# First piece's transposes at a phase end set between the third bank's products, and the transposes of C dealt 8 clock units later

## The chip, the cores and the metric

The kernel runs on one core of a Trainium2 chip. The metric is the device time of one execution in microseconds; of several executions the median is given. TensorE is called PE in the profile, VectorE DVE, ScalarE ACT, GpSimd POOL and SyncE SP.

## The reference, cut to what matters

Two layers work on 256 tokens of width 1024, all in float32. A layer adds half a SwiGLU feed-forward block (width 2816) to h, then a token mixer, then half of a second SwiGLU block. The mixer of the first layer is an S5 diagonal state-space layer, that of the second is block-sparse attention with 8 heads, which for 256 tokens is plain causal attention.

```
def reference(x, ...):
    h = x
    for layer in range(DEPTH):
        h = h + 0.5 * swiglu(rms_norm(h, ffn_norm[layer, 0]), ...)
        hn = rms_norm(h, mix_norm[layer])
        if layer % 2 == 0: h = h + s5_mixer(hn, ...)
        else:              h = h + moba_mixer(hn, ...)
        h = h + 0.5 * swiglu(rms_norm(h, ffn_norm[layer, 1]), ...)
    return h
```

The S5 layer has 64 groups of 16 channels and 64 complex states each; its matrices B and C, the powers of its diagonal and tables made of them depend on weights alone.

## The kernel before, in words

**Phases.** The work is six phases in a row, named f00, s5, f01, f10, moba and f11: four feed-forward blocks and the two mixers. Every phase reads h transposed (model width on partitions) and ends by adding its result to h. Both stand in SBUF.

**Products in three passes.** Each float32 operand is split into a rounded high part and the rest, in a format that PE multiplies at full rate, and each product is three matmuls: high by high, high by low, low by high (`mm3`, L398 to L401; L553 to L555 in the feed-forward phases after the first). The weights stream through the class `Stream`: a `raw` buffer (three of them) is filled by a DMA of SP; a *split* makes `whi` on ScalarE (L86, or L92 with the norm's gains) and `wlo` on VectorE (L87, L93). Up to nine halves of such split weights are held. `st.pump()` issues the next split if a place is free, `st.release` frees a place.

**Order.** The instructions of each engine run in the order in which the program issues them; there is no scheduler. An engine stops at an instruction whose inputs or whose buffer are not ready, and everything behind it on that engine waits too.

**A phase end.** The function `boundary` ends a phase. The result is four accumulators (PSUM banks, `pA`), one for each 128x512 piece of h: two token tiles t by two halves n of the width. The pieces are ended in an order that the next phase sets. In the feed-forward phases the last products come in three parts of three matmuls for each piece; in s5 and moba in two parts of six. The first two pieces get all parts but the last ahead of time. Then for each piece come the parts that are left, `finish` (L371, VectorE: h gets the accumulator times a scale), and the transposes of a piece for the next phase, `prep`: four 128x128 transposes by PE into a PSUM bank `pR` (L333), a copy by ScalarE to the high part (L335), a subtraction by VectorE for the low part (L336), and the squares for the norm on ScalarE (L345). There are two `pR` banks, taken in turn by every transpose of the kernel. `prep` of the last piece comes in the next phase. After s5, a `pump` follows the second and the third piece.

**The front.** During the first phase, f00, the tables of the S5 layer are built beside the feed-forward products. A counter of *clock units* is advanced by `fill` ahead of PE's products: 0.7 for each three matmuls, so 5.6 for a gate/up product of one token tile and 2.8 for a down product. The generator `tables` issues its pieces by that clock: loads at the units in `LOADS`, the powers E from unit `E_AT`, B from `B_AT`, and the four blocks of transposes of C from unit `C_AT`, 1.4 units apart. A block is four transposes by PE into a `pR` bank (L830) and two copies by ScalarE into the table `cb` (L833):

```
later = [(C_AT + 1.4 * k, c_tr) + divmod(k, 2) for k in range(4)]
...
if later and later[0][0] <= now:
    f = later.pop(0)
    f[1](*f[2:])
    done[0] += 1
```

The tables that are made of C wait in the program until all four blocks have been issued (`done`). In f00 the activations are transposed too: twice in the course of a gate/up pair, two 128x128 transposes into a `pR` bank (L497), with a copy by ScalarE (L499) and a subtraction by VectorE (L500).

Of the kernel before, what the change touches and what calls it, by code (L numbers as in the profile page):

```python
# [30 lines left out]
OO = 68  # L31

LOADS = (20, 21, 22, 23, 24, 26, 28, 30, 32, 34, 36, 38) + (44, 50, 56, 66, 76, 88, 100, 112)
C_AT, E_AT, B_AT, DENSE, LAG, PACE, AGE = 44, 26, 36, (64, 0.39, 0.46), 12, 3.5, 8.0


class Stream:
# [83 lines left out]
def trunk_kernel(ctx: ExitStack, tc, x, ffn_norm, ffn_w_gate, ffn_w_up, ffn_w_down, mix_norm,  # L121
# [17 lines left out]
    def psR():  # L139
        return pp.tile([128, 512], F32, name="pR", tag="R", bufs=2)  # L140
# [176 lines left out]
    def home(pool, ph):  # L317

        xa = pool.tile([128, 4224], F32R, name="xa")
        v = xa[:, XO[ph]:XO[ph] + 4096].rearrange("p (i k c) -> p i k c", i=2, c=256)  # L320
        return v[:, 0], v[:, 1]

    def prep(t, n, ph, sq=True):

        if (ph, "x") not in X:
            X.clear()
            X[ph, "x"] = True
            X["h"], X["l"] = home(XP[0], ph)
        hh = h[t][:, n * 512:(n + 1) * 512]
        ps = psR()  # L330
        pv = ps.rearrange("p (k c) -> p k c", c=128)
        for k in range(4):
            nc.tensor.transpose(pv[:, k, :], hh[:, k * 128:(k + 1) * 128], ident)  # L333
        xh, xl = (X[p][:, n * 4:n * 4 + 4, t * 128:t * 128 + 128] for p in "hl")
        nc.scalar.activation(xh, pv, AF.Copy)  # L335
        nc.vector.tensor_tensor(xl, pv, xh.bitcast(F32), op=OP.subtract)  # L336
        if sq:
            squares(t, n)

    def squares(t, n):  # L340
        if n == 0:
            SS[t] = sp.tile([128, 2], F32, name="ss", tag="ss", bufs=4)
        hh = h[t][:, n * 512:(n + 1) * 512]
        sq = sp.tile([128, 512], mybir.dt.bfloat16, name="sq", tag="sq", bufs=1)
        nc.scalar.activation(sq, hh, AF.Square, accum_out=SS[t][:, n:n + 1])  # L345
        if n == 1:
            v = sp.tile([128, 1], F32, name="ms", tag="ms", bufs=4)
            nc.gpsimd.tensor_tensor(v, SS[t][:, 0:1], SS[t][:, 1:2], op=OP.add)  # L348
            nc.gpsimd.tensor_scalar(v, v, 1.0 / D, EPS, op0=OP.mult, op1=OP.add)
            r = sp.tile([128, 1], F32, name="rr", tag="rr", bufs=4)  # L350
            rsq(r, v, 1)
            Rr[t] = r
# [16 lines left out]
    def finish(t, n, acc, scale):  # L369
        hh = h[t][:, n * 512:(n + 1) * 512]  # L370
        nc.vector.scalar_tensor_tensor(hh, acc, scale, hh, op0=OP.mult, op1=OP.add)  # L371

    def boundary(nxt, parts, acc, scale, mid=None, pumps=()):

        if nxt is not None and nxt[0] == "f":
            order = [(0, 0), (1, 0), (0, 1), (1, 1)]
        else:
            order = [(0, 0), (0, 1), (1, 0), (1, 1)]
        for i in range(2):
            for part in parts[:-1]:  # L380
                part(*order[i])
            if mid is not None and i == 0:
                mid()
        for i, (t, n) in enumerate(order):
            for part in parts[-1:] if i < 2 else parts:
                part(t, n)
            finish(t, n, acc[2 * t + n], scale)
            if nxt is None:
                store(t, n)
            elif i:  # L390
                prep(*order[i - 1], nxt)
            if i in pumps:
                st.pump()
# [33 lines left out]
    def store(t, n):  # L427
        hh = h[t][:, n * 512:(n + 1) * 512]
        for s in range(4):
            off, ap = rows(t, s, n)  # L430
            (nc.sync, nc.scalar)[s % 2].dma_start(bass.AP(tensor=out.tensor, offset=out.offset + off, ap=ap),
                                                  hh[s * 32:s * 32 + 32])


    def ffn(tag, nxt, hooks, fill, to_rows, to_columns):
# [91 lines left out]
        def part(j, f):  # L527
            return lambda t, n: bank_mm(acc, t, n, *AT[j], where[tag, "d", j], [f], False, (j, f) == (L, 1))

        boundary(nxt, [part(L - 1, 1), part(L, 0), part(L, 1)], acc, 0.5, lambda: tr(L, 1))  # L530
        st.release(where[tag, "d", L - 1], 1)
        for i in range(2):
            st.release(where[tag, "d", L], i)

    def ffn_w(tag, nxt, entry):
# [75 lines left out]
        def part(j, f):  # L611
            return lambda t, n: bank_mm(acc, t, n, *AT[j], where[tag, "d", j], [f], False, (j, f) == (L, 1))

        boundary(nxt, [part(L - 1, 1), part(L, 0), part(L, 1)], acc, 0.5)
        st.release(where[tag, "d", L - 1], 1)
        for i in range(2):
# [359 lines left out]
    def s5(nxt, entry):  # L976
# [209 lines left out]
        for word in plan.split():  # L1186
            step(word)
        boundary(nxt, [lambda t, n: so(2, t, n), lambda t, n: so(3, t, n, True)], acc, 1.0, pumps=(1, 2))
        for b in (2, 3):
            for i in range(2):  # L1190
# [246 lines left out]
    for i, ph in enumerate(phases):  # L1437
        nxt = phases[i + 1] if i + 1 < len(phases) else None
# [59 lines left out]
```

## Time and profile before

| what | value |
|---|---|
| median of 3 runs | 975.3 us (974.68 to 975.59) |
| the profiled execution | 974.58 us |
| its span, first to last instruction | 972.8 us |
| mean granted TensorE clock | 0.999 |
| PE, PE weight loads | 965.9 us (99%), 863.7 us (89%) |
| DVE, ACT, POOL | 690.1 us (71%), 555.7 us (57%), 211.6 us (22%) |
| mean DMA rate | 207 GB/s |

In a row of a timeline stand the start, the duration, the engine, the line of the program, the operation, out<-in, shapes and the count of merged instructions; in brackets the idle time of the engine before it and the instruction that ended it. A matmul's record is longer than the step to the next one, since matmuls overlap; its end is modelled. In a row of the view of waits stand who waited for whom, the microseconds in total, the times and the longest. A group of instructions of one line has its count, the durations in ns (smallest, median, largest) and the first and last start.

### The profile page before, as it was taken

Reading aid. Unit: us, or ns where it says so; the run is one execution under the profiler, and the core shown is the slowest. Engines: PE = TensorE matmul, PEld = TensorE weight load, DVE = VectorE, ACT = ScalarE, POOL = GpSimd, SP = SyncE. Lnnn points to the kernel's source line nnn. Section 1 sums busy time; section 2 is a strip of 40 time slices with the busy share of each in tenths; the row PEclk is TensorE's granted clock in tenths of the full one; section 3 lists DMA queues with packets and bytes.
Section 4 is the critical chain, followed back from the end, with each engine's and each line's share of the span. In section 5 each row is a group of like instructions: output and inputs, shape, how many; then the busy total and the mean of one; then the engine's idle time right before and its main releaser. Section 6 shows DMA issues by size and latency. Waiting matters only on the chain.

```text
span 972.8 us, 17168 instructions
## 1 busy us (share of the span) xinstructions
PE 965.9 (99%) x6695; PEld 863.7 (89%) x6695; DVE 690.1 (71%) x1118; ACT 555.7 (57%) x1008; POOL 211.6 (22%) x381
## 2 busy tenths in 40 slices
PE   9999999999999999999999999999999999999998
PEld 7878777888999999999899999998888899999997
DVE  5898778768886776666568766665688667766662
ACT  7655767553376565555356555554897556555540
POOL 5961889615702000000020000001440020000000
PEclk9999999999999999999999999999999999999999
DMA  8999999986756666555446755553454646656531
GB/s 287 255 308 311 286 278 289 287 298 225 269 196 194 217 198 220 182 187 184 156 134 226 241 181 186 182 194 95 171 173 131 215 132 216 220 182 207 173 131 43
DMA packets 145505, 200.91 MB, mean 207 GB/s; under 512 B 20153, under 2 KB 117521, under 8 KB 145169
## 3 DMA queue, kind: packets, MB, share of 16 engines
q1 hardware_dynamic: 138032, 188.51, 59.4%
q0 software_dynamic: 6816, 10.71, 4.2%
q8 instruction: 52, 0.85, 0.4%
q10 hardware_dynamic: 576, 0.61, 0.3%
q14 instruction: 29, 0.23, 0.1%
HBM read 183.89 MB, written 15.76 MB: 205 GB/s over the span
## 4 chain that ended last, share of the span: by engine, by line
PE 94%; DVE 3%; POOL 2%; issue 0%; ACT 0%; ACTq 0%; POOLq 0%
PE pM L554 13%; PE pM L553 13%; PE pM L555 13%; PE pA L399 9%; PE pA L401 9%; PE pA L400 9%; PE pM L399 6%; PE pM L400 6%; PE pM L401 6%; PE pR L1066 1%; DVE wlo L87 1%; PE pR L333 1%; POOL sc L686 1%; PE pA L1110 1%; PE pA L1112 1%; PE pA L473 1%
## 5 line engine op out<-in xcount | busy, mean ns | idle before, releaser
L553 PE MATMUL pM<-xa,whi 128*128 128x256 f32 x1056 | 295.7, 280 | 0.0
L554 PE MATMUL pM<-xa,whi 128*128 128x256 f32 x1056 | 294.9, 279 | 0.0
L555 PE MATMUL pM<-xa,wlo 128*128 128x256 f32 x1056 | 294.7, 279 | 0.0
L93 DVE SCALAR_TENSOR_TENSOR wlo<-raw,gT,whi 128x512 fp32r<-128x512 f32 x328 | 228.0, 748 | 68.9 <-ACT whi L92 68.7
L87 DVE TENSOR_TENSOR wlo<-raw,whi 128x1024 fp32r<-128x1024 f32 (+1 forms) x155 | 189.2, 1234 | 48.7 <-ACT whi L86 47.1
L92 ACT ACTIVATE whi<-raw,gT 128x512 fp32r<-128x512 f32 x328 | 213.7, 712 | 14.9 <-PE pA L401 14.8
L554 PEld LDWEIGHTS pM<-xa,whi 128*128 128x128 f32 x1056 | 198.5, 188 | 2.6
L553 PEld LDWEIGHTS pM<-xa,whi 128*128 128x128 f32 x1056 | 198.5, 188 | 2.3
L555 PEld LDWEIGHTS pM<-xa,wlo 128*128 128x128 f32 x1056 | 198.5, 188 | 0.0
L86 ACT ACTIVATE whi<-raw 128x1024 fp32r<-128x1024 f32 (+1 forms) x155 | 159.5, 1049 | 31.4 <-DMA raw<-in_ffn_w_up_dram 13.1
L399 PE MATMUL pA<-whi,ah 128*128 128x512 f32 x352 | 138.7, 394 | 0.0
L400 PE MATMUL pA<-wlo,ah 128*128 128x512 f32 x352 | 137.6, 391 | 0.0
L401 PE MATMUL pA<-whi,al 128*128 128x512 f32 x352 | 137.6, 391 | 0.0
L399 PE MATMUL pM<-whi,xa 128*128 128x512 f32 (+1 forms) x304 | 122.1, 402 | 0.0
L568 ACT ACTIVATE sg<-gr 128x256 f32<-128x256 f32 x66 | 27.6, 419 | 164.4 <-DVE gr L565 164.4
L400 PE MATMUL pM<-wlo,xa 128*128 128x512 f32 (+1 forms) x304 | 115.8, 381 | 0.1
L401 PE MATMUL pM<-whi,xa 128*128 128x512 f32 (+1 forms) x304 | 115.4, 380 | 0.0
L348 POOL TENSOR_TENSOR ms<-ss 128x1 f32<-128x1 f32 x10 | 1.9, 193 | 471.8 <-ACT sq L345 471.8
L401 PEld LDWEIGHTS pA<-whi,al 128*128 128x128 f32 x352 | 66.1, 188 | 14.3
L399 PEld LDWEIGHTS pA<-whi,ah 128*128 128x128 f32 x352 | 66.1, 188 | 11.6
L400 PEld LDWEIGHTS pA<-wlo,ah 128*128 128x128 f32 x352 | 66.2, 188 | 11.4
L565 DVE TENSOR_TENSOR gr<-pM,rrow 128x512 f32<-128x512 f32 x66 | 45.5, 690 | 39.4 <-PE pM L555 39.3
(271 smaller groups left out, 1230.6 us busy)
## 6 DMA issues: line engine op xcount, KB each, us to landing
raw<-in_ffn_w_down_dram SPq DMA_DIRECT2D x44, 1024.0 KB, 5.6
raw<-in_ffn_w_gate_dram SPq DMA_DIRECT2D x80, 512.0 KB, 4.0
raw<-in_ffn_w_up_dram SPq DMA_DIRECT2D x80, 512.0 KB, 5.1
raw<-in_moba_w_qkv_dram SPq DMA_DIRECT2D x12, 1024.0 KB, 5.1
TB<-dB SPq DMA_DIRECT2D x8, 768.0 KB, 6.7
raw<-in_ffn_w_gate_dram SPq DMA_DIRECT2D x16, 256.0 KB, 4.4
raw<-in_ffn_w_up_dram SPq DMA_DIRECT2D x16, 256.0 KB, 4.7
dA<-blank SPq DMA_DIRECT2D x8, 512.0 KB, 9.2
```

The lines of the kernel that those rows point to most:

```text
L86: nc.scalar.activation(hi[:, c], r[:, c], AF.Copy)
L87: nc.vector.tensor_tensor(lo[:, c], r[:, c], hi[:, c].bitcast(F32), op=OP.subtract)
L92: nc.scalar.activation(hi[:, c], r[:, c], AF.Identity, scale=g)
L93: nc.vector.scalar_tensor_tensor(lo[:, c], r[:, c], g, hi[:, c].bitcast(F32), op0=OP.mult, op1=OP.subtract)
L399: mm(o, xh, wh, start=start, stop=False)
L400: mm(o, xh, wl, start=False, stop=False)
L401: mm(o, xl, wh, start=False, stop=stop)
L553: mm(o, a, xh, start=k == 0 and i == 0, stop=False, skip_group_check=True)
L554: mm(o, a, xl, start=False, stop=False, skip_group_check=True)
L555: mm(o, b, xh, start=False, stop=k == 7, skip_group_check=True)
L565: V.tensor_tensor(gr, ps.rearrange("p (i c) -> p i c", i=2), Rr["row"][:, None, :].to_broadcast([128, 2, 256]), op=OP.mult)
L568: nc.scalar.activation(sg, gr[:, 0, :], AF.Silu)
```

## The change

Two edits. In `boundary`, the transposes of the first piece are no longer issued behind the second piece's last part and `finish`, but behind the first part of the third piece, so three matmuls later at the end of a feed-forward phase and six at the end of s5 and moba. The transposes of the second and third piece stay where they were. At the end of the kernel (`nxt` is None) nothing is transposed. And `C_AT` is 52 for 44, so the four blocks of transposes of C are issued one gate/up product and one down product later, at the same places in them.

```
-C_AT, E_AT, B_AT, DENSE, LAG, PACE, AGE = 44, 26, 36, (64, 0.39, 0.46), 12, 3.5, 8.0
+C_AT, E_AT, B_AT, DENSE, LAG, PACE, AGE = 52, 26, 36, (64, 0.39, 0.46), 12, 3.5, 8.0
...
         for i, (t, n) in enumerate(order):
-            for part in parts[-1:] if i < 2 else parts:
+            for k, part in enumerate(parts[-1:] if i < 2 else parts):
                 part(t, n)
+                if i == 2 and k == 0 and nxt is not None:
+                    prep(*order[0], nxt)
             finish(t, n, acc[2 * t + n], scale)
             if nxt is None:
                 store(t, n)
-            elif i:
+            elif i > 1:
                 prep(*order[i - 1], nxt)
             if i in pumps:
                 st.pump()
```

On PE the moved blocks are all that changes its order. On ScalarE the copies of C move with them, past the splits and the activations of the stage between; and at the end of s5 one split comes ahead of the first piece's copy and squares; there VectorE's two operations of that split come ahead of the first piece's subtraction. VectorE's order elsewhere, and the orders of POOL and SP, are as before. Two lines are added, so a line behind `boundary` has a number higher by two in the changed kernel (L399 is L401, L500 is L502, L830 is L832).

More of the change, by code (lines that the diff above doesn't have):

```diff
@@ L33 @@
 LOADS = (20, 21, 22, 23, 24, 26, 28, 30, 32, 34, 36, 38) + (44, 50, 56, 66, 76, 88, 100, 112)
-C_AT, E_AT, B_AT, DENSE, LAG, PACE, AGE = 44, 26, 36, (64, 0.39, 0.46), 12, 3.5, 8.0
+C_AT, E_AT, B_AT, DENSE, LAG, PACE, AGE = 52, 26, 36, (64, 0.39, 0.46), 12, 3.5, 8.0
 class Stream:
@@ L384, in boundary @@
         for i, (t, n) in enumerate(order):
-            for part in parts[-1:] if i < 2 else parts:
+            for k, part in enumerate(parts[-1:] if i < 2 else parts):
                 part(t, n)
+                if i == 2 and k == 0 and nxt is not None:
+                    prep(*order[0], nxt)
             finish(t, n, acc[2 * t + n], scale)
@@ L389, in boundary @@
                 store(t, n)
-            elif i:
+            elif i > 1:
                 prep(*order[i - 1], nxt)
```

## The prediction

> **What bounds the kernel now.** I read the page's busy times first, then the chain that ended last, then TensorE's waits, and last the timelines of the places that the change touches.
>
> ```profile
> PE 965.9 (99%) x6695; PEld 863.7 (89%) x6695; DVE 690.1 (71%) x1118; ACT 555.7 (57%) x1008; POOL 211.6 (22%) x381
> PE 94%; DVE 3%; POOL 2%; issue 0%; ACT 0%; ACTq 0%; POOLq 0%
> ```
>
> TensorE (PE) is busy for 965.9 of 972.8 us and carries 94% of the chain. No product and no transpose is added or dropped by the change, so it can win only what PE now waits at the moved places, and can lose only by new waits of PE. What does PE wait for? First its row in the view of waits, then the answer on line 333 (transposes of h), whose second row says what PE's weight loads or matmuls stood idle for:
>
> ```profile
> PE pR L830 <- DVE al L500: 0.8, 1, 0.8
> L333 PE MATMUL pR<-cst,h x80: 270/272/330, 204.1 to 784.9; 128*128 128x128 f32 x80
>   DVE h L371: 1.6, 3
> ```
>
> Both lines are the moved ones: one wait at the transposes of C (L830), three at those of h. Some of these idle times count the load and the matmul of one wait twice, and a matmul's end is modelled, so I price each from the starts of the products around it.
>
> **Part 1: the first piece's transposes at the phase ends.** At a phase end the four 128x512 pieces of h are finished one after another. Before, piece 1's transposes come right behind the second piece's last product. PE at the end of the first phase: the passage with the wait, then the second piece's transposes (the row between is left out), which do not wait; below them the waiting passages of the two other phase ends:
>
> ```profile
> 203.63 0.39 PE L401 MATMUL pA<-whi,al 128*128 128x512 f32 x1
> 204.12 0.66 PE L333 MATMUL pR<-cst,h 128*128 128x128 f32 x4
> 204.53 0.48 PE L399 MATMUL pA<-whi,ah 128*128 128x512 f32 x1
> ...
> 206.46 0.40 PE L401 MATMUL pA<-whi,al 128*128 128x512 f32 x1
> ...
> 207.05 0.48 PE L399 MATMUL pA<-whi,ah 128*128 128x512 f32 x1
> ...
> 483.23 0.39 PE L401 MATMUL pA<-whi,al 128*128 128x512 f32 x1
> ...
> 484.14 0.48 PE L399 MATMUL pA<-whi,ah 128*128 128x512 f32 x1
> ...
> 669.63 0.39 PE L401 MATMUL pA<-whi,al 128*128 128x512 f32 x1
> ...
> 670.54 0.48 PE L399 MATMUL pA<-whi,ah 128*128 128x512 f32 x1
> ```
>
> From the last product before to the first after: 0.90 us with the wait, 0.59 without; 0.91 and 0.91 at the two others. That is 0.31 + 0.32 + 0.32 = 0.95 us in three phase ends. The cause is VectorE's add into h (L371), two of them in one row:
>
> ```profile
> 203.37 1.38 DVE L371 SCALAR_TENSOR_TENSOR h<-pA,h 128x512 f32<-128x512 f32 x2 [1.22 <-PE pA L401]
> 206.89 0.69 DVE L371 SCALAR_TENSOR_TENSOR h<-pA,h 128x512 f32<-128x512 f32 x1 [0.76 <-PE pA L401]
> ```
>
> The first add ends at about 203.37 + 0.69 = 204.06. In the changed order three products stand between, so the transposes come up at 203.63 + 4 x 0.23 = 204.55, some 0.5 us after the add: the wait goes. (0.23 is the step from one product to the next, 70.75 to 70.98 in the rows of part 2.)
>
> What is late next? The second piece's transposes come six products later, with their add done by 204.75. For piece 1, transposes (0.6), ScalarE's copy (0.6, as in a row below) and VectorE's subtraction (an operation of the add's size, 0.7) are through at 204.55 + 1.9 = 206.5. Behind it VectorE has the third piece's add, which PE releases no sooner than 206.89 - 0.31 = 206.58. And the transposes' PSUM buffer (there are two, in turn) is wanted again by the third piece's transposes at 207.05 - 0.31 + 9 x 0.23 = 208.8. So nothing takes the wait's place.
>
> A rule to weigh here: the Trainium skill, "TensorE: Matmul & The Clock Gate", section "Step-by-step: what each phase is for", says that PE's queue pulls weight loads ahead of running matmuls. By that rule a block that waits loses its hidden load too; counting late starts alone (0.49 against 0.23 us) would give 0.26 a place and 0.17 us less in all. The whole passages measured above agree with the rule, and I use them.
>
> The two other phase ends (after the state-space and the attention layer) have six products ahead of the transposes and no wait:
>
> ```profile
> 295.79 0.39 PE L401 MATMUL pA<-whi,xa 128*128 128x512 f32 x1
> ...
> 296.38 0.48 PE L399 MATMUL pA<-whi,xa 128*128 128x512 f32 x1
> ```
>
> 295.79 to 296.38 is again 0.59, so they bring 0. After the state-space layer one weight split (two ScalarE and two VectorE operations) now comes ahead of piece 1's copies in both queues:
>
> ```profile
> 296.71 0.60 ACT L335 ACTIVATE xa<-pR 128x512 fp32r<-128x512 f32 x1 [6.39 <-issue]
> 297.81 1.33 ACT L92 ACTIVATE whi<-raw,gT 128x512 fp32r<-128x512 f32 x2
> ```
>
> ScalarE had been idle for 6.39 us, so the split can run there. If it ran no earlier than before (297.81 to 299.14), piece 1's copy would begin at 299.1 instead of 296.7; PE asks for that PSUM buffer again only at the third piece's transposes, 24 products and a block behind 296.38, near 302.3. So it costs 0 either way. The kernel's last phase end transposes nothing and is unchanged.
>
> **Part 2: the transposes of C, 8 clock units later.** They are four blocks (L830) of four transposes. PE at the second block, without a wait, and at the fourth:
>
> ```profile
> 56.00 0.39 PE L401 MATMUL pM<-whi,xa 128*128 128x512 f32 x1
> 56.23 0.60 PE L830 MATMUL pR<-cst,cn 128*64 128x128 f32 x4
> 56.59 0.48 PE L399 MATMUL pM<-whi,xa 128*128 128x512 f32 x1
> 56.90 0.39 PE L400 MATMUL pM<-wlo,xa 128*128 128x512 f32 x1
> ...
> 60.54 0.39 PE L401 MATMUL pA<-whi,al 128*128 128x512 f32 x1
> 61.68 0.63 PE L830 MATMUL pR<-cst,cn 128*64 128x128 f32 x4 [0.75 <-DVE al L500]
> 62.06 0.48 PE L399 MATMUL pA<-whi,ah 128*128 128x512 f32 x1
> 62.38 0.39 PE L400 MATMUL pA<-wlo,ah 128*128 128x512 f32 x1
> ```
>
> A block costs 0.90 - 2 x 0.23 = 0.44 us, wherever it stands. The fourth takes 62.38 - 60.54 = 1.84, so its wait is 0.94 us: it needs the PSUM buffer that a transpose of the activations filled, and VectorE, behind with the table of powers and the splits, subtracts from it (L500) only at 61.21:
>
> ```profile
> 61.21 0.41 DVE L500 TENSOR_TENSOR al<-pR,ah 128x256 fp32r<-128x256 f32 x1
> 63.24 0.79 DVE L628 TENSOR_TENSOR e<-z,z 128x256 f32<-128x256 f32 x2
> 65.48 1.23 DVE L87 TENSOR_TENSOR wlo<-raw,whi 128x1024 fp32r<-128x1024 f32 x1 [0.76 <-ACT whi L86]
> 70.10 0.42 DVE L500 TENSOR_TENSOR al<-pR,ah 128x256 fp32r<-128x256 f32 x1
> ```
>
> Each block moves exactly one gate/up product and one down product on, and the fourth again stands behind the first bank of the down product, in the buffer of an activation transpose. So the same wait can come back there. PE and ScalarE around that place:
>
> ```profile
> 68.70 0.38 PE L497 MATMUL pR<-cst,act 128*128 128x128 f32 x2
> 70.75 0.39 PE L401 MATMUL pA<-whi,al 128*128 128x512 f32 x1
> 70.98 0.39 PE L399 MATMUL pA<-whi,ah 128*128 128x512 f32 x1
> 64.39 1.06 ACT L86 ACTIVATE whi<-raw 128x1024 fp32r<-128x1024 f32 x1 [1.28 <-PE pA L401]
> 67.52 1.06 ACT L86 ACTIVATE whi<-raw 128x1024 fp32r<-128x1024 f32 x1 [0.30 <-PE pM L401]
> L833 ACT ACTIVATE cb<-pR x8: 360/377/379, 56.6 to 62.7; 64x256 f32<-64x256 f32 x8
> ```
>
> When PE reaches the product that follows the 64.39 row it is 4 x 0.44 + 0.94 = 2.70 us earlier than before. The fourth block comes up at 70.98 - 2.70 + 3 x 0.44 = 69.60. Before, L500 began 70.10 - 65.48 = 4.62 us after the first split of that stretch, and that split waited for ScalarE, which waited for PE. ScalarE's wait moves 2.70 earlier with PE (64.39 to 61.7), VectorE is free from 64.03 on, so the split begins at about 64.2 and L500 is through at 64.2 + 4.62 + 0.42 = 69.2: 0.4 us in hand. ScalarE has two pairs of C copies more between its splits (2 x 0.377 = 0.75 us each). First block: twelve products ahead of the activation transposes, 68.70 - 2.70 - 12 x 0.23 = 63.2; second: 63.2 + 0.44 + 6 x 0.23 = 65.1; each done some 0.6 later. So ScalarE has split one at 61.7 to 62.8, the first pair at 63.9, split two at 64.6, the second pair at 65.7, split three from 66.5 to 67.5, which VectorE needs at 69.2 - 0.42 - 1.2 = 67.6. That fits. The cost lies between 0 and 0.94; I take 0, by the rows of that stretch, in which VectorE stands idle for 0.76 us.
>
> The weights have more in hand: the split at 65.48 is first used by PE one whole gate/up product later, at
>
> ```profile
> 75.77 0.39 PE L399 MATMUL pM<-whi,xa 128*128 128x512 f32 x1
> 66.00:203.00 137.00, 137.00 (x742) 110.35 (x741) 107.87 (x151) 84.02 (x144) 81.10 (x103) 1.00 0.96 285
> ```
>
> 9 us after it is ready. The second row (windows by stage; the last columns are granted clock 1.00, DMA share 0.96, GB/s) shows PE busy for all of the 137 us that follow, with DMA full at 0.96.
>
> **Sum.** 0.95 + 0.94 = 1.89 us less. The profiled execution has 974.58 us, 1.8 of it around the span of 972.8; it would have 972.7. It lies 0.7 below the median of the runs, so against 975.3 the forecast is 973.4, or 0.19%. What a measurement of this kernel can tell from no change is about 0.2%, here 1.95 us: the forecast lies at that line.
>
> **Rivals.** *A: the front's wait returns.* The fourth block waits at its new place, as VectorE's chain (third split, then L500) does not come 1.3 us earlier. The bound is L500 staying at 70.52: 70.52 - 69.60 = 0.92 us, and with it the front's gain is gone: 974.3. For it: the place has the same form as before. Against it: 0.76 us of idle VectorE. The Trainium skill, "Perfetto Trace Analysis", section "Optimization Strategy", takes a repeating gap on the engine that should be saturated as a sign of too few buffers; by that rule moving the block moves the gap, and the two-deep transpose buffer would give this case. The trace bears it out only in part: three of the four blocks pass without a gap. Chance 0.10.
>
> *B: the transfers swallow the front's gain.* With DMA at 0.96 up to 203 us, PE that is 0.94 earlier could wait for weights or for the state-space tables: 974.3. Against it: 9 us in hand at 75.77 and no wait of PE in those 137 us. Chance 0.05.
>
> *C: slower.* The C copies now stand in ScalarE's queue ahead of the activation copy that L500 needs. If VectorE's order slips by all of them, L500 ends at 70.52 + 1.5 = 72.0 and PE waits 2.4 us at the fourth block: 2.4 - 1.89 = 0.5 above before, 975.8; if the later splits slip as well, more. It decides once L500 ends after 69.60 + 1.89 = 71.5. Against it: ScalarE is idle 1.28 and 0.30 us before the two splits quoted. Chance 0.07.
>
> **How the numbers follow.** The forecast has 0.78. Its centre is 0.06 us short of the 0.2% line, and the three runs shown (974.68 to 975.59) lie further below their median than above, so I split it nearly evenly: 0.43 beyond the line, 0.35 within. A and B fall within (0.15). C gives slower: 0.07, taken whole though its first price is short of the line. Faster 0.43, same 0.50, slower 0.07. The range takes the forecast less the whole scatter of the runs, 0.9, and reaches up to A and B with half of it, 0.4: 972.5 to 974.7.
>
> **What would show it.** Right: no wait of line 333 for h in the three phase ends, and each passage 0.59 us or less by its starts; the fourth L830 block with no idle time before it, near 69.6; the first phase end's transposes of h at 204.55 - 0.94 = 203.6. Wrong: an idle time in brackets at the fourth L830 naming L500, a wait of PE for a split or a table after it, or a span that ends less than 1.5 us earlier.

## The result, and the profile after

| | before | after |
|---|---|---|
| median of 19 runs each, on the same chip | 975.21 us | 972.94 us (972.39 to 975.6) |
| the profiled execution | 974.58 us | 972.72 us |
| its span | 972.8 us | 970.9 us |
| mean granted TensorE clock | 0.999 | 1.000 |

The ratio is 0.9976, with a 95% interval of 0.9969 to 0.9983, so the kernel is faster, by 0.17 to 0.31%. By the medians that is 2.27 us less (0.23%), by the profiled executions 1.86. The forecast was 973.4, in a range of 972.5 to 974.7.

The page after, in its line of busy times; then PE's whole answer in the view of waits, and the group of line 333 (the rows on transposes of h):

```profile
span 970.9 us, 17168 instructions
PE 964.9 (99%) x6695; PEld 863.7 (89%) x6695; DVE 690.0 (71%) x1118; ACT 555.3 (57%) x1008; POOL 211.7 (22%) x381
...
PE pR L1394 <- POOL ones L229: 1.0, 1, 1.0
...
L333 PE MATMUL pR<-cst,h x80: 270/272/273, 203.7 to 783.1; 128*128 128x128 f32 x80
```

PE has as many instructions as before. The row of L830 (now L832) is gone from PE's waits: the one left stands at the very start of the kernel, before its first matmul at 0.98 us, and was there before too. Line 333 has no row of idle time any more, and its longest transpose takes 273 ns where one took 330. Now the three phase ends by their starts, in the timeline of PE after; the first row of each stretch is the second piece's last product, behind which the transposes stood before:

```profile
202.81 0.39 PE L403 MATMUL pA<-whi,al 128*128 128x512 f32 x1
...
203.49 0.39 PE L403 MATMUL pA<-whi,al 128*128 128x512 f32 x1
203.73 0.60 PE L333 MATMUL pR<-cst,h 128*128 128x128 f32 x4
204.08 0.48 PE L401 MATMUL pA<-whi,ah 128*128 128x512 f32 x1
...
482.05 0.39 PE L403 MATMUL pA<-whi,al 128*128 128x512 f32 x1
...
482.73 0.39 PE L403 MATMUL pA<-whi,al 128*128 128x512 f32 x1
...
483.31 0.48 PE L401 MATMUL pA<-whi,ah 128*128 128x512 f32 x1
...
668.12 0.39 PE L403 MATMUL pA<-whi,al 128*128 128x512 f32 x1
...
668.80 0.39 PE L403 MATMUL pA<-whi,al 128*128 128x512 f32 x1
...
669.38 0.48 PE L401 MATMUL pA<-whi,ah 128*128 128x512 f32 x1
```

From the product before the transposes to the one behind them: 204.08 - 203.49 = 0.59, 483.31 - 482.73 = 0.58, 669.38 - 668.80 = 0.58 us, where the waiting passages took 0.90, 0.91 and 0.91.

The same rows tell where the time went. The second piece's last product started at 203.63, 483.23 and 669.63 before; it is 0.82, 1.18 and 1.51 us earlier now. The kernel's last product (L401 at 967.66 before, L403 after) closes the account. Two products in PE's timeline before:

```profile
50.10 0.39 PE L401 MATMUL pM<-whi,xa 128*128 128x512 f32 x1
967.66 0.39 PE L401 MATMUL pA<-whi,al 128*128 128x512 f32 x1
```

The same two in PE's timeline after:

```profile
50.20 0.39 PE L403 MATMUL pM<-whi,xa 128*128 128x512 f32 x1
965.85 0.39 PE L403 MATMUL pA<-whi,al 128*128 128x512 f32 x1
```

At 50 us, ahead of everything that the change touches, the profiled execution after is 0.10 us later. Its shift then goes +0.10, -0.82, -1.18, -1.51, -1.81. So the front gave 0.92 us and the three phase ends 0.36, 0.33 and 0.30, all of it at the four predicted places.

The front after, by PE's timeline (the fourth block of C), VectorE's and ScalarE's:

```profile
69.46 0.39 PE L403 MATMUL pA<-whi,al 128*128 128x512 f32 x1
69.69 0.60 PE L832 MATMUL pR<-cst,cn 128*64 128x128 f32 x4
...
70.36 0.39 PE L402 MATMUL pA<-wlo,ah 128*128 128x512 f32 x1
...
64.30 1.21 DVE L87 TENSOR_TENSOR wlo<-raw,whi 128x1024 fp32r<-128x1024 f32 x1
...
68.91 0.41 DVE L502 TENSOR_TENSOR al<-pR,ah 128x256 fp32r<-128x256 f32 x1
...
61.77 1.06 ACT L86 ACTIVATE whi<-raw 128x1024 fp32r<-128x1024 f32 x1 [2.25 <-PE pA L403]
63.97 0.77 ACT L835 ACTIVATE cb<-pR 64x256 f32<-64x256 f32 x2 [1.14 <-PE pR L832]
64.76 1.06 ACT L86 ACTIVATE whi<-raw 128x1024 fp32r<-128x1024 f32 x1
65.78 0.77 ACT L835 ACTIVATE cb<-pR 64x256 f32<-64x256 f32 x2
66.57 1.06 ACT L86 ACTIVATE whi<-raw 128x1024 fp32r<-128x1024 f32 x1
```

The fourth block's passage takes 70.36 - 69.46 = 0.90 us, as long as that of the second block, which did not wait before. VectorE's subtraction is through at 68.91 + 0.41 = 69.32, and the block comes up at 69.69: 0.37 us in hand.

### The profile page after: what moved, and what is told of

The parts are those of the page before. It is cut to its first block, busy times and chain, and to the rows that moved or that the text cites. A ratio compares the mean times of both kernels' runs of the same rounds, so it can differ in the third digit from the quotient of the medians.

```text
span 970.9 us, 17168 instructions
## 1 busy us (share of the span) xinstructions
PE 964.9 (99%) x6695; PEld 863.7 (89%) x6695; DVE 690.0 (71%) x1118; ACT 555.3 (57%) x1008; POOL 211.7 (22%) x381
## 4 chain that ended last, share of the span: by engine, by line
PE 94%; POOL 2%; issue 2%; DVE 1%; ACT 1%; POOLq 0%; ACTq 0%
PE pM L556 13%; PE pM L555 13%; PE pM L557 13%; PE pA L401 10%; PE pA L403 10%; PE pA L402 10%; PE pM L401 6%; PE pM L402 5%; PE pM L403 5%; PE pR L1068 1%; PE pA L475 1%; POOL qrs L306 1%; PE pR L333 1%; PE pA L1112 1%; PE pA L1114 1%
## 5 line engine op out<-in xcount | busy, mean ns | idle before, releaser
L92 ACT ACTIVATE whi<-raw,gT 128x512 fp32r<-128x512 f32 x328 | 213.5, 711 | 14.9 <-PE pA L403 14.9
L401 PE MATMUL pA<-whi,ah 128*128 128x512 f32 x352 | 138.7, 394 | 0.0
L403 PE MATMUL pA<-whi,al 128*128 128x512 f32 x352 | 137.6, 391 | 0.0
L401 PE MATMUL pM<-whi,xa 128*128 128x512 f32 (+1 forms) x304 | 122.2, 402 | 0.0
L403 PE MATMUL pM<-whi,xa 128*128 128x512 f32 (+1 forms) x304 | 115.4, 380 | 0.0
L403 PEld LDWEIGHTS pA<-whi,al 128*128 128x128 f32 x352 | 66.1, 188 | 14.3
L401 PEld LDWEIGHTS pA<-whi,ah 128*128 128x128 f32 x352 | 66.1, 188 | 11.7
```

Source lines behind the costliest of these rows:

```text
L92: nc.scalar.activation(hi[:, c], r[:, c], AF.Identity, scale=g)
L401: mm(o, xh, wh, start=start, stop=False)
L403: mm(o, xl, wh, start=False, stop=stop)
```

## The experiments

**Both edits again, and each alone.** The first is the changed kernel once more, the second has only the phase ends (`C_AT` back at 44), the third only the front (`boundary` as before, `C_AT` 52).

> The changed kernel again, beside the other three. Theory (PE's four waits go and nothing takes their place): span 1.9 us shorter than before, about 970.9, time about 1.9 to 2.3 us less. If the extra 0.4 us between the timed runs (2.27 us) and the spans (1.9 us) is real, it shows again here; if it is scatter, the difference falls near 1.9.

> Only the transposes of h are moved, C stays at 44. Theory: the three waits at phase ends go (0.33 + 0.32 + 0.32), the wait of 0.94 us at the fourth block of C stays: span 971.8, about 1.0 us less than before. Rival (the phase ends' waits come back behind the move): span 972.8.

> Only C_AT is 52, the phase ends are as before. Theory: the front's wait goes and is not given back in the 137 us of full DMA queues that follow: span 971.9, about 0.9 us less. Rival B (the transfers swallow it): products are 0.9 us earlier at 75 us, but no longer at 200 us, span 972.8. If the parts add up, this and the kernel with the transposes of h alone give together what the whole change gives.

| kernel | median, us | ratio to before (975.06), 95% |
|---|---|---|
| both | 972.91 | 0.998 (0.997 to 0.999) |
| phase ends alone | 974.08 | 0.9989 (0.998 to 0.9998) |
| front alone | 973.92 | 0.9987 (0.9978 to 0.9996) |

The parts bring 0.98 and 1.14 us, together 2.12; both bring 2.15. Each of these intervals is about 0.9 us wide on either side, so the medians alone would not show that the parts add up; the traces do. By the starts of the same products the phase ends alone go from 0.20 us later than before at 203 us to 0.77 earlier at the last product, a gain of 0.97, and the front alone goes from 0.18 later at 50 us to 0.74 earlier at 100 us, a gain of 0.92. Together that is 1.89, beside 1.91 for both edits. Neither takes the other's gain. With the front alone line 333 keeps its idle time (1.6 us in three waits for h, as before). With the phase ends alone the wait in the front stays; here is the fourth block in PE's timeline with the phase ends alone:

```profile
60.36 0.39 PE L403 MATMUL pA<-whi,al 128*128 128x512 f32 x1
61.88 0.63 PE L832 MATMUL pR<-cst,cn 128*64 128x128 f32 x4 [1.13 <-DVE al L502]
...
62.58 0.39 PE L402 MATMUL pA<-wlo,ah 128*128 128x512 f32 x1
```

The passage takes 62.58 - 60.36 = 2.22 us, where the profile of before has 1.84, though up to here the program is the same: PE came 0.18 us earlier than in that profile, and VectorE's subtraction was through 0.20 us later. The wait of 0.94 us was 1.32 in this execution.

With the front alone the starts of the same products are 0.74 us earlier at 100 us and still 0.74 earlier at 960 us. What the front gains, nothing later takes back in this profile: rival B falls.

**The fourth block alone.** Is it enough to move the block that waited? Here `boundary` is as before, and of the four blocks only the last one is issued later:

```
later = [(c, c_tr) + divmod(k, 2) for k, c in enumerate((44.0, 45.4, 46.8, 56.2))]
```

> Phase ends as before; of the four blocks of C only the fourth is issued 8 clock units later, the first three stay. Theory: only the fourth block cost anything, by its wait for the PSUM buffer, so this alone brings the same 0.9 us: span 971.9. Rival (it is the crowd of four blocks in one stretch that puts PE behind VectorE): a quarter to a half of it, span 972.3 to 972.6.

974.04 us, 0.9989 (0.9981 to 0.9998): 1.02 us less than before, as much as all four together (1.14) within what can be told apart. In its profile PE waits at none of the four blocks; the same products gain 0.91 us between 54 and 100 us. (This one profile loses 0.4 us again up to 223 us, 0.2 of it at one place at 150 us; the profile with all four blocks moved does not, and the median does not show it.) The other three need not have moved.

**Two blocks left at the old place.** Two readings of the old wait are left: four blocks crowd ScalarE and VectorE at that place, or a block there takes a `pR` bank whose turn comes too early. If it is the crowd, fewer blocks wait less; if it is the turn, what counts is which of the two banks the last block there draws. In the changed kernel, two and then only one of the blocks go back:

```
later = [(c, c_tr) + divmod(k, 2) for k, c in enumerate((46.8, 48.2, 54.8, 56.2))]   # two
later = [(c, c_tr) + divmod(k, 2) for k, c in enumerate((48.2, 53.4, 54.8, 56.2))]   # one
```

> The changed kernel, but two blocks of C are issued at clock units 46.8 and 48.2, the places of the third and fourth block of before, and two at 54.8 and 56.2. Theory (the wait comes from the turn of the two transpose buffers: the block at 48.2 gets the buffer of the activation transposes, which VectorE empties only at 61.5 to 61.9): with two blocks fewer ahead PE arrives there 0.9 us earlier than before, at about 59.9, and waits 1.8 us, twice as long as before; span 970.9 + 1.8 = 972.7. Rival (crowding): with half the blocks the wait is at most half: span 971.4 or less.

> The changed kernel, but one block of C is issued at clock unit 48.2, where the fourth of before stood, and the other three at 53.4, 54.8 and 56.2. Theory (turn of the buffers): alone there, it gets the other buffer, which has been free since 54.7, and does not wait, although it comes up even earlier (about 59.5) and VectorE is as late as ever: span 970.9. Rival (any transpose of C at that place waits for VectorE): a wait of 1.8 to 2.2 us, span about 973.

Two blocks: 975.05 us, 1.0002 (0.9993 to 1.0012), beside 974.79 before, so the whole gain of both edits is gone. One block: 972.92 us, 0.9987 (0.9977 to 0.9996), so most of the gain stays: 1.87 us by the medians. PE's and VectorE's timelines with two blocks at the old place:

```profile
59.81 0.39 PE L403 MATMUL pA<-whi,al 128*128 128x512 f32 x1
62.01 0.63 PE L832 MATMUL pR<-cst,cn 128*64 128x128 f32 x4 [1.81 <-DVE al L502]
62.39 0.48 PE L401 MATMUL pA<-whi,ah 128*128 128x512 f32 x1
...
61.54 0.41 DVE L502 TENSOR_TENSOR al<-pR,ah 128x256 fp32r<-128x256 f32 x1
```

And with one, at the same place of the program:

```profile
58.84 0.39 PE L403 MATMUL pA<-whi,al 128*128 128x512 f32 x1
59.07 0.60 PE L832 MATMUL pR<-cst,cn 128*64 128x128 f32 x4
59.43 0.48 PE L401 MATMUL pA<-whi,ah 128*128 128x512 f32 x1
...
60.88 0.41 DVE L502 TENSOR_TENSOR al<-pR,ah 128x256 fp32r<-128x256 f32 x1
```

With half the blocks the wait is twice as long: 62.39 - 59.81 = 2.58 against 0.58 us, so 2.0 us lost where the four lost 0.94. PE arrives earlier, as less stands ahead of it, and VectorE's subtraction ends no earlier for that. With one block the subtraction is as late against PE (it starts 1.8 us after the block), and PE does not wait at all. By the order of the program the first block behind the transposes of the activations draws the other bank, and the second block draws theirs, which VectorE's subtraction has yet to read. The single block is a first one. So the wait is one for a bank's turn. Crowding falls. The run with only the fourth block moved fits this: there the third block at the old place, and the fourth at the new one, are both the first behind such transposes.

**ScalarE's copies of C doubled.** Rival C was a new wait at the new place, from copies of C in ScalarE's queue. To see how near it is, each copy is made twice (the same data to the same place):

```
-            for g in range(2):
+            for g in (0, 1, 0, 1):
```

> The changed kernel with each pair of ScalarE copies of the transposed C done twice (the same data again). It tests how thin the cover of the new place is (rival C of the prediction). Theory: the second pair ends at about 68.0 instead of 66.6, so the third block, which wants that buffer at 67.2, waits about 0.8 us, and the subtraction ahead of the fourth ends at about 70.7, another 0.2: span 970.9 + 1.0 = 971.9. Rival (the new place has ample cover): span 970.9.

974.3 us, 0.9996 (0.9987 to 1.0006): 1.4 us more than the kernel with one block at the old place, measured beside it (972.92), and more than the 1.0 expected. PE's timeline, third and fourth block:

```profile
67.16 0.38 PE L499 MATMUL pR<-cst,act 128*128 128x128 f32 x2
68.34 0.62 PE L832 MATMUL pR<-cst,cn 128*64 128x128 f32 x4 [0.81 <-ACT cb L835]
68.72 0.48 PE L401 MATMUL pM<-whi,xa 128*128 128x512 f32 x1
...
70.65 0.39 PE L403 MATMUL pA<-whi,al 128*128 128x512 f32 x1
...
71.54 0.48 PE L401 MATMUL pA<-whi,ah 128*128 128x512 f32 x1
```

The third block's passage takes 68.72 - 67.16 = 1.56 us where the changed kernel has 0.57, the fourth's 71.54 - 70.65 = 0.89 where it has 0.58: together 1.30. The larger part is at the third block: the banks are taken in turn, the transposes of the activations at 67.16 stand between it and the second block, so it draws the second block's bank, of which ScalarE now makes four copies. That wait, 0.99 us, is not the one rival C named. C's own, the activations' subtraction that comes late behind the copies, is the smaller part, 0.31 us at the fourth block: the subtraction is through at 70.97 where the changed kernel has 69.32. The change stays short of both waits, and not by much: its second pair of copies is through at 65.78 + 0.77 = 66.55, and the third block comes up at 67.19.

**One product instead of three.** How far must the first piece's transposes be moved? Here they stand behind the first of the third piece's three products:

```
             for k, part in enumerate(parts[-1:] if i < 2 else parts):
+                if i == 2 and k == 0 and nxt is not None:
+                    INNER.append(lambda: prep(*order[0], nxt))
                 part(t, n)
-                if i == 2 and k == 0 and nxt is not None:
-                    prep(*order[0], nxt)
...
     def mm3(o, xh, xl, wh, wl, start, stop):
         mm(o, xh, wh, start=start, stop=False)
+        while INNER:
+            INNER.pop()()
```

> The changed kernel with the first piece's transposes behind the first product of the third piece instead of the third. Theory (only VectorE's add has to be over): they come up 0.46 us after the last product's start, the add is visible 0.49 us after it, so 0.03 us of wait are left at each of the three feed-forward ends: span 971.0. Rival (the transposes need the longer distance, by the weight loads pulled ahead): up to 0.2 us at each, span 971.5.

973.33 us, 0.9987 (0.9977 to 0.9996), where three products had 972.9 in other sets of runs. The group of line 333 and PE's timeline at the first phase end:

```profile
L333 PE MATMUL pR<-cst,h x80: 270/272/329, 203.2 to 783.4; 128*128 128x128 f32 x80
...
  DVE h L371: 0.9, 3
...
202.92 0.40 PE L403 MATMUL pA<-whi,ah 128*128 128x512 f32 x1
203.18 0.66 PE L333 MATMUL pR<-cst,h 128*128 128x128 f32 x4
203.59 0.48 PE L406 MATMUL pA<-wlo,ah 128*128 128x512 f32 x1
```

The three waits come back, smaller: 203.59 - 202.92 = 0.67 us, 0.08 more than the 0.59 without a wait, where I expected 0.03. One more product (0.23 us) would have covered that; it was not tried.

**A next step: four waits in the attention layer.** With the waits of this change gone, PE's weight loads still wait for VectorE's splits four times in the attention layer; it did so before the change too (1.8 us in four). The view of waits of PE's weight loads after, and the first such place in PE's timeline:

```profile
PEld pM L402 <- DVE wlo L93: 1.9, 4, 0.5
...
687.89 0.39 PE L401 MATMUL pM<-whi,xa 128*128 128x512 f32 x1
688.35 0.50 PE L402 MATMUL pM<-wlo,xa 128*128 128x512 f32 x1
688.69 0.39 PE L403 MATMUL pM<-whi,xa 128*128 128x512 f32 x1
```

Two steps take 0.46 and 0.34 us in place of 0.23 each, so about 0.34 us is lost. In VectorE's queue the rotary operations on q and k (`rope`), which wait for GpSimd (0.95 us ahead of this place), stand ahead of the split that PE needs. The slots of that layer are dealt by `at(slot, ...)`; one slot more puts `rope` behind the split. First for all eight q and k products, beside the changed kernel:

```
-                at(4 * (i + 1) + 2, rope, *prods[i])
+                at(4 * (i + 1) + 3, rope, *prods[i])
```

> The changed kernel with one more edit, in the attention layer: VectorE's rotary operations are issued one place later, behind the next weight split and no longer ahead of it. In the changed kernel's trace PE still waits four times for such a split, 1.9 us in the view of waits, and by the starts of neighbouring products about 0.3 us each. Theory: the four waits go and the attention layer is about 1.2 us shorter, about 971.8 us; nothing before 660 us changes. Rival: the rotary operations, which come later, now hold up the transposes of q and k or the scores, and nothing or less than half is gained (972.5 to 973.5).

> The changed kernel itself once more, beside the one with the later rotary operations. Theory: 972.9 us, and 1.9 to 2.3 us less than before; its profile tells whether the differences of a few tenths between single profiles (at the start and in the state-space layer) come back.

975.14 us with all eight, 1.0001 (0.9993 to 1.001); the changed kernel has 972.9, 0.9975 (0.9966 to 0.9985), beside the same 975.13 of before. The rival won, and the loss is beyond its range of 972.5 to 973.5. The largest of PE's waits with all eight; VectorE's split ahead of the seventh product's `rope`, in its timeline:

```profile
PE pR L1255 <- DVE sm L1284: 1.9, 2, 1.3
...
723.70 1.42 DVE L93 SCALAR_TENSOR_TENSOR wlo<-raw,gT,whi 128x512 fp32r<-128x512 f32 x2 [1.13 <-ACT whi L92]
```

Two waits for 1.9 us came up at the transposes of q and k (L1255). By the starts of the same products it had gained 0.82 us on the changed kernel up to 715 us, and from there to 735 us it lost 3.1. Up to the fifth product the edit was right; behind it the softmax shares the queues. The row names L1284, its reciprocal, but what the transposes read is written by `rope`, which ends just ahead of it. `rope` now stands behind a split for which VectorE waits 1.13 us for ScalarE (L92), and ScalarE's queue has the softmax's exponentials there. So the seventh product's `rope` begins at 725.03, where the changed kernel has 723.14. Which of the softmax's operations makes ScalarE late was not tested. So the edit for the first five alone:

```
+                at(4 * (i + 1) + (3 if i < 5 else 2), rope, *prods[i])
```

> The changed kernel with the rotary operations one place later for the first five of the eight q and k products only. With all eight later, PE was 0.8 us ahead of the changed kernel at 715 us (from the same start-up) and lost about 3.1 us after that, between 715 and 735, at the transposes of the last three. Theory: the gain of the first five stays and the loss goes: 0.6 to 0.8 us less than the changed kernel, 972.1 to 972.3 us, and two waits of PE for such a split are left in place of four. Rival: the wait at the fifth or sixth product comes back larger, and the kernel is no faster than the changed one (972.9 us or more).

971.79 us, 0.9972 (0.996 to 0.9984): 3.2 us less than before, and 1.1 less than the changed kernel's medians, of which its profile shows 0.9 by the starts of the same products (0.02 us earlier at 660, 0.92 to 0.93 from 720 to the end); 0.6 to 0.8 was expected. By its interval it beats the kernel of before. It was not measured beside the changed kernel, so what it gains on that one rests on the 0.9 us of its profile. One such wait is left, where two were expected; in the timeline of weight loads:

```profile
728.32 0.19 PEld L402 LDWEIGHTS pM<-wlo,xa 128*128 128x128 f32 x1 [0.47 <-DVE wlo L93]
```

Its median comes from 6 runs, so its distance from the changed kernel's median is less sure than the ratio to before.

## Why the prediction was right, point by point

**The phase ends** (forecast 0.95, measured 0.36 + 0.33 + 0.30 = 0.99 by the starts of products). The transposes of h at the first end were forecast at 203.6 and stand at 203.73, 0.10 of which is the late start. Nothing took the wait's place there: line 333 has no idle time at all. The kernel with one product shows that it was the distance from VectorE's add that cleared it. The place where one weight split now comes ahead of piece 1's copy cost nothing, by the first of the two readings. ScalarE's timeline after:

```profile
287.82 2.55 ACT L92 ACTIVATE whi<-raw,gT 128x512 fp32r<-128x512 f32 x4
296.89 0.60 ACT L335 ACTIVATE xa<-pR 128x512 fp32r<-128x512 f32 x1 [6.53 <-issue]
```

Four operations, two splits, run together at 287.82 (before, two), inside the time in which ScalarE stood idle, and the copy follows PE at 296.89. The shift there stays as it was: the forecast of 0 held for the ends of s5 and of the attention layer.

**The front** (forecast 0.94, measured 0.92). The steps came out close: split one at 61.77 (forecast 61.7), the first pair of copies at 63.97 (63.9), VectorE's split behind it at 64.30 (64.2), split two at 64.76 (64.6), the second pair at 65.78 (65.7), split three at 66.57 (66.5), the subtraction through at 69.32 (69.2), the fourth block at 69.69 (69.60), with 0.37 us in hand (0.4). VectorE's idle 0.76 us ahead of a split was the cover, as argued. Rival A, the wait that comes back at a place of the same form, did not happen, and the runs with two blocks and with one tell why the form alone doesn't decide: what counts is whose bank a block draws, and when VectorE frees it. The Trainium skill's rule that was quoted for that rival ("Perfetto Trace Analysis", "Optimization Strategy": a repeating gap can mean too few buffers) agrees as far as a bank's turn was the cause, by the wait of 1.81 us with two blocks; but one block moved was enough here, with as few buffers as before.

**The sum** (forecast 1.89). The profiled executions differ by 974.58 - 972.72 = 1.86 us. That part was right to a few hundredths, and so close a fit of two single executions has luck in it: two other profiles of the changed kernel have spans 0.5 and 1.0 us longer (last section).

**What was mis-sized** is the step from the profiled execution to the median. I carried over 0.7 us, by which the profiled execution of before lay below the median of three runs. The profiled one of after lies 972.94 - 972.72 = 0.22 below its median. So the median is 972.94 and not 973.4. The medians differ by 2.27, 2.15 and 2.23 us in three sets of runs, some 0.3 more than the four places explain. What these 0.3 us are stays open. One candidate is on record: the old wait in the front was 0.94 us in the profile from which it was priced and 1.32 in the profile with the phase ends alone, so the forecast may have started from a small one. With 1.32 the four places give 2.3 us. But that is one execution against another, and the timed runs have no trace, so it is only argued. The drift of the last section was seen only in kernels with both edits, and would make the difference smaller. The interval of the first set, 0.0017 to 0.0031 of 975.2 or 1.7 to 3.0 us, holds 1.89.

**The chances.** The forecast said that the result would lie at the line of 0.2%, and gave 0.43 to a result beyond it and 0.50 to one within. The median lies a little beyond, at 0.23%; the interval of 0.17 to 0.31% has zero outside and the line inside, so on which side of the line the gain lies is not settled. Rival C did not come, but doubled copies brought 1.3 us of waits, 0.31 of them C's own, so a cover of 0.37 us was worth a chance.

## What to carry to other kernels

Price a wait by the starts of the instructions around it, with the wait and without, and move the waiting work as far as that price asks: three products (0.68 us) in between made waits of 0.31 us vanish here, and one product (0.23 us) left 0.08 of each. Where buffers are used in turn, ask whose turn a moved or removed user changes: of four blocks at one place, leaving two there made the wait twice as long, and leaving one made it vanish. A gain of a few tenths is read from the shift of the same instruction between two traces, stage by stage; the difference of two spans mixes it with whatever else the two executions lost. And a wait that is priced from one execution is one sample: the front's was 0.94 us in one and 1.32 in another.

## What the runs showed that I had not expected

Two executions of the same program can differ by almost a microsecond at one place. Of the changed kernel there are three profiles, with spans of 970.9, 971.4 and 971.9 us. The last differs from the first in one wait, in the state-space layer. There PE waits for ScalarE, whose operation starts at 256.32 in the first. PE's and ScalarE's timelines in the third:

```profile
257.92 0.34 PE L1068 MATMUL pR<-U,TB 128*64 128x64 f32 x4 [0.69 <-ACT gf L1094]
...
257.48 0.39 ACT L1094 ACTIVATE gf<-pR 128x256 f32<-128x256 f32 x1 [1.05 <-DVE xa L1087]
```

ScalarE is 1.16 us later here. By the starts of the same products the third profile is 0.01 us behind the first at 240 us, and 0.93 to 0.95 behind it from 290 us to the end. The second profile has the same wait, smaller: 0.4 us by the starts of products. It is in the profiles of the kernels with two blocks, with one block and with doubled copies too, and in neither profile of before and after. The changed kernel has it in two of its three profiles, so it hangs on the execution. But it was seen in five of the nine profiles of kernels with both edits in some form, and in none of the four others, so the runs do not rule out that the edits make it likelier. What makes ScalarE wait there was not followed up. With the start-up, which was up to 0.45 us later in one profile than in that of before, it is why single spans tell nothing below a microsecond here.
